# A chunked scan on one core: spilt activations asked for two chunks sooner

## The chip, the cores and the metric

The kernel runs on one core of one Trainium2 chip. The metric is the device time of an execution in microseconds; lower is better. TensorE is called PE here, VectorE DVE, ScalarE ACT, GpSimd POOL and SyncE SP, as in the profile.

## The reference, cut to what matters

A trunk of two layers over 1024 tokens of width 1024, all in float32: a causal spatial-gating layer, then a Mamba-2 SSD layer, then a norm. The change lies in the second layer, whose scan works on 8 groups of 4 heads, in chunks of 128 tokens:

```python
proj = h @ w_in                                   # z | xbc | dt
xbc = silu(causal_depthwise_conv(xbc, conv_w, conv_b))
x, Bm, Cm = split(xbc)                            # in chunks of 128 tokens, 8 groups
dA_cs = cumsum(softplus(dt_raw + dt_bias) * A)    # within a chunk
cb = einsum('bclgn,bcsgn->bclsg', Cm, Bm)
w_ls = cb * exp(dA_cs[l] - dA_cs[s]) (causal) * dt
y_diag = einsum('bclsgj,bcsgjp->bclgjp', w_ls, x)
states = einsum('bclgn,bclgj,bclgjp->bcgjpn', Bm, decay_to_end * dt, x)
prev = scan over chunks: carry * chunk_decay + states
y_off = einsum('bclgn,bcgjpn,bclgj->bclgjp', Cm, prev, exp(dA_cs))
y = y_diag + y_off + x * d_skip
out = rmsnorm_per_group(y * silu(z)) @ w_out      # h = h + out, then the final norm
```

## The kernel before, in words

Large products are made of float32 operands that are split in a high and a low part, three matmuls each (`mm3`, L134 to L136). The order of the work is written out by hand: what stands earlier in the Python text stands earlier on each engine, and a buffer's next user waits for its last reader.

The projections of the second layer come first. For four of the eight groups (`SPILT = (0, 1, 3, 5)`) the convolved x, B and C (`xbc`) are computed ahead of the scan and stored to DRAM, in `xbc_d` of the group, half by half: a **half** is 4 chunks, so there are 16 of them, and half H is group H // 2, with chunks 4H to 4H + 3 in a count n that runs from 0 to 63 over all groups. The projections of the other four groups (`projections`, matmuls into `ab`) are interleaved with the scan as filler: `project` moves them on by a share that grows evenly with n.

`scans` is the loop over the 64 chunks. For each chunk n it puts, in this order: `own` and `off` (PE: this chunk's state and the carried state's part, into `os`), at an even n also `diagonal` for the chunks n and n + 1 (PE, into `yy`) and the loads of the decay matrices `wl` for n + 4 and n + 5 (L1590, on SP; they take the buffers which the diagonal has just read, so they wait for PE), a share of the projections, `pe_a(n + 3)` (PE: three transposes and a product into `tp`, L1595 and L1596, the first that reads a half's `xbc`), then the state's update, the decays (ACT, L1601 and L1603), the weights (DVE, L1619), the skip term (DVE, L1676, of n and n + 1 at an even n), the sum and the gate (POOL, L1689). At a half's end its squares are taken (ACT, L1700), `z` gated is stored (`g_d`, L1704) and a sum of squares is stored (`ss_d`, L1720).

`prefetch(g, th, part)` asks for a half's data on SP's queue. Part 0 is the 1 MB of `xbc` (L1555), for a spilt group only. Part 1 is `ze`: `z` (L1559) and four broadcasts of the decays `ecs_d` (L1563). Part 0 of half H + 1 is asked for at the end of chunk 4H, part 1 at the end of chunk 4H + 1, in which `pe_a` already takes chunk 4H + 4. Both use the pool `s8` with 16 buffers of 8 KB in each partition, which the projections' results, the operands of the products (`hh`, `hl`) and the scan's halves share in turn.

SP issues its DMAs in the order written, and an issue that waits for a buffer holds those behind it. Eight counters of finished DMAs go round, so that a DMA also waits for the one that had its counter before.

The functions that the change touches:

Of the kernel before, what the change touches and what calls it, by code (L numbers as in the profile page):

```python
# [29 lines left out]
def kernel(  # L30
# [34 lines left out]
    def s8(shape, name, dt=F32):  # L65
        return sb.tile(shape, dt, name=name, tag="s8", bufs=16)
# [1244 lines left out]
    def convolve():  # L1311

        finish()
        if todo:
            late.append(todo.pop(0)())
# [75 lines left out]
    def drain(n=1):  # L1391

        for _ in range(min(n, len(queue))):
            for f in queue.pop(0):
                f()
# [153 lines left out]
    def prefetch(g, th, part):  # L1549

        st = sts[g]
        if part == 0:
            if g in xbc_d:
                t = st["xbc", th] = s8([P, 4, 512], "xbc")
                nc.sync.dma_start(out=t, in_=xbc_d[g][:, th])  # L1555
            return
        ze = st["ze", th] = s8([P, 4, 512], "ze")
        if g < G - 1:
            nc.sync.dma_start(out=ze[:, 0:2], in_=z_d[g][:, :, th * 512:(th + 1) * 512])  # L1559
        for f in range(2):  # L1560
            for pt in range(2):
                h = 4 * g + 2 * pt + f
                nc.sync.dma_start(out=ze[f * 64:(f + 1) * 64, 2 + pt],  # L1563
                                  in_=ecs_d[h, th * 512:(th + 1) * 512].partition_broadcast(64))
# [158 lines left out]
    def group_rstd(g, t0, n):  # L1723


        c = n // P
        sv = tiny([P, 8], "sv")[:, 0:c]
        nc.sync.dma_start(out=sv, in_=ss_d[g, t0:t0 + n].rearrange("(p c) -> p c", c=c))
        got = []

        def guess():
            nc.vector.tensor_scalar(sv, sv, 1.0 / 256, NORM_EPS, ALU.mult, ALU.add)
            got.append(rsqrt_a(sv, c))

        def tail():
            rv = tiny([P, 8], "rvv")[:, 0:c]
            rsqrt_b(rv, sv, got[0], c)
            got.append(rv)

        def put():  # L1740
            nc.sync.dma_start(out=rs_d[g, t0:t0 + n].rearrange("(p c) -> p c", c=c), in_=got[1])

        return guess, tail, put
# [117 lines left out]
    def scans():  # L1861


        chunks = [(g, c) for g in range(G) for c in range(8)]
        N, M = len(chunks), 50
        scan, rs, ran = {}, {}, [0]
        total = 32 * len(plain)

        def fill():
            yield from pj  # L1870
            yield from bo.product(1, hook_b)

        fl = fill()

        def project(upto):
            while ran[0] < upto:
                next(fl, None)
                ran[0] += 1

        def want(at):  # L1880
            if at < M:
                return AHEAD + (total - AHEAD) * at // M
            return total + min(16 * (at - M) // (N - 5 - M), 16 + 2 * (at - N + 5))

        def at(f, n, *a):
            if 0 <= n < N:
                g, c = chunks[n]
                if g not in scan:
                    scan[g] = Scan(g, nc.gpsimd)
                getattr(scan[g], f)(c, *a)  # L1890

        prefetch(0, 0, 0), prefetch(0, 0, 1)
        project(AHEAD // 2 + 1)
        while todo or late:
            convolve()
        for n in range(4):
            at("load", n)
        drain(1)
        for n in range(2):
            at("decay", n)  # L1900
        drain(len(queue))
        at("pe_a", 0), at("tokens", 0), at("weights", 0)
        at("pe_a", 1), at("tokens", 1), at("weights", 1)
        drain(len(queue))
        project(AHEAD)
        at("decay", 2)
        at("pe_a", 2), at("tokens", 2)
        for n, (g, c) in enumerate(chunks):
            if n == M + 3:
                drain(len(queue))  # L1910
            elif n == N - 9:
                for k in range(2):
                    bo.get("a", 0, 0, k)
            elif n == N - 7:
                end["scan"] = scan[G - 1]
                bo.get("b", 0, 0, 0)
            p = g if c >= 4 else g - 1
            if c % 2 == 0:
                at("own", n), at("off", n)
                at("diagonal", n)  # L1920
                if c % 4 == 0 and g > 0:
                    scan[g - 1].sum_b()
                elif n == N - 2:
                    scan[g].sum_b(n=2)
                at("load", n + 4), at("load", n + 5)
                project(want(n + .5))
                at("pe_a", n + 3)
                at("update", n)
                at("carry", n + 1)
                at("weights", n + 2)  # L1930
                at("decay", n + 3)
                at("skip", n)
                at("out", n)
                at("skip", n + 1)
                drain()
                at("tokens", n + 3)
                at("gate", n)
                if c % 4 == 0 and g > 0:
                    scan[g - 1].sum_c(1 if c else 0)
                drain()  # L1940
            else:
                at("own", n), at("off", n)
                project(want(n + .5))
                at("pe_a", n + 3)
                at("update", n)
                at("carry", n + 1)
                at("weights", n + 2)
                at("out", n)
                drain()
                at("decay", n + 3)  # L1950
                at("tokens", n + 3)
                at("gate", n)
                drain()
            if n >= N - 7:
                k = n - N + 7
                if k % 2:
                    bo.prep(1, k // 2)
                else:
                    bo.ready(0, 0, k // 2)
            th = 0 if c >= 4 else 1  # L1960
            if p >= 0:
                sc = scan[p]
                if p == G - 1:
                    if c == 4:
                        sc.gate_half(th), sc.squares(th)
                elif c % 4 == 0:
                    sc.squares(th)
                elif c % 4 == 1:
                    sc.store(th)
                    sc.sum_a()  # L1970
            if g > 0:
                if c == 6:
                    rs[g] = group_rstd(g - 1, 0, T)
                elif c == 7:
                    rs[g][0]()
            if c == 0 and g > 1:
                rs[g - 1][1]()
            if c == 1 and g > 1:
                rs[g - 1][2]()
            k = n + 4  # L1980
            if c % 4 < 2 and k < N:
                prefetch(k // 8, k // 4 % 2, c % 4)
            project(want(n + 1))
        sc = scan[G - 1]
        for k in (0, 1):
            bo.get("a", 0, 1, k)
        bo.get("b", 1, 0, 0)
        sc.sum_c(0), rs[G - 1][1](), rs[G - 1][2]()
        bo.prep(1, 3)
        sc.gate_half(1), sc.squares(1)  # L1990
        end["half"] = [group_rstd(G - 1, 0, 512)]
        for k in (0, 1):
            bo.get("a", 1, 0, k)
        while ran[0] < total + 31:
            project(ran[0] + 1)
        sc.sum_b(n=2)
        sc.sum_c(1)
        for _ in fl:
            pass
# [22 lines left out]
    with tc.manual_schedule():  # L2022
        scans()
        into_end()
# [28 lines left out]
```

## Time and profile before

| what | us |
| --- | --- |
| three runs | 1519.4, 1520.2, 1528.06 |
| median | 1520.2 |
| the profiled execution | 1520.27 |
| its span in the trace | 1518.6 |

The span starts with the program's first instruction. The scan's chunks run from about 1007 us (first transposes) to 1346 us (last); the output projection fills the rest. Waits are listed as: engine, line and tile that waited, what it waited for, total us, times, longest. In a timeline a row has start, duration, engine, line, operation, tiles, shapes, and in brackets the idle time of the engine before it and what ended it; `SPq` is an issue on SP's queue. A row of stretches has the stretch, its length, the busy time of PE, PEld (weight load), DVE, ACT and POOL with the instructions in it, the granted PE clock, the DMA engines' share and GB/s.

### The profile page before, as it was taken

What the parts mean: (1) busy time and instruction counts of PE and PEld (TensorE: products, weight loads), DVE (VectorE), ACT (ScalarE), POOL (GpSimd) and SP (SyncE); (2) the same over time, 40 slices, a digit from 0 to 9 for tenths busy, and PEclk for the clock granted to TensorE, in tenths of its full rate; (3) what the DMA queues carried; (4) which work ended last, traced back from release to release, by engine and by line L of the source; (5) the groups of instructions that cost most, each with busy time, mean ns of one, the idle gap of its engine ahead of it and who ended that gap; (6) DMA issues with size and microseconds to landing.
All of it is one profiled execution on the core that took longest, in us unless ns stands there. A gap on an engine that the chain in (4) does not pass through costs nothing. (4 is left out here: it accounts for less than half of the span.)

```text
span 1518.6 us, 21342 instructions
## 1 busy us (share of the span) xinstructions
PE 1463.4 (96%) x7834; PEld 1230.3 (81%) x7834; DVE 1049.1 (69%) x1713; ACT 784.2 (52%) x1256; POOL 402.0 (26%) x451
## 2 busy tenths in 40 slices
PE   6899999999999999999999999998999989999997
PEld 6899988888888888877878888877787878777875
DVE  7966566676666655678657467766677767688876
ACT  6533332232322445556666566565766676756463
POOL 1111110000000023202131313126666676642221
PEclk9999999999999999999999999999999999999999
DMA  5554323322322999948377888776656555589972
GB/s 183 140 169 143 106 89 108 110 105 101 116 87 79 361 247 243 257 133 163 112 174 161 182 169 162 153 235 188 180 145 191 166 181 140 159 264 276 250 162 111
DMA packets 174952, 254.45 MB, mean 168 GB/s; under 512 B 16400, under 2 KB 103168, under 8 KB 171648
## 3 DMA queue, kind: packets, MB, share of 16 engines
q1 hardware_dynamic: 124768, 168.93, 36.0%
q0 software_dynamic: 42448, 70.27, 23.0%
q10 hardware_dynamic: 7632, 13.90, 2.5%
q8 instruction: 62, 1.02, 0.3%
q14 instruction: 42, 0.34, 0.1%
HBM read 186.14 MB, written 51.18 MB: 156 GB/s over the span
## 5 line engine op out<-in xcount | busy, mean ns | idle before, releaser
L134 PE MATMUL acc<-hh,wh 128*128 128x512 f32 x868 | 340.1, 392 | 0.8 <-ACT u L296 0.8
L136 PE MATMUL acc<-hh,wl 128*128 128x512 f32 x868 | 338.5, 390 | 1.9 <-DVE wl L112 1.8
L135 PE MATMUL acc<-hl,wh 128*128 128x512 f32 x868 | 337.8, 389 | 0.0
L112 DVE TENSOR_TENSOR wl<-wr,wh 128x1024 fp32r<-128x1024 f32 (+1 forms) x96 | 114.3, 1192 | 118.7 <-ACT wh L111 118.6
L136 PEld LDWEIGHTS acc<-hh,wl 128*128 128x128 f32 x868 | 162.9, 188 | 37.8 <-DVE wl L112 3.6
L134 PEld LDWEIGHTS acc<-hh,wh 128*128 128x128 f32 x868 | 163.1, 188 | 35.0 <-ACT u L296 1.8
L135 PEld LDWEIGHTS acc<-hl,wh 128*128 128x128 f32 x868 | 163.0, 188 | 33.2
L296 ACT COPY u<-acc 128x512 f32<-128x512 f32 x115 | 66.9, 583 | 197.8 <-PE acc L136 197.7
L111 ACT CAST wh<-wr 128x1024 fp32r<-128x1024 f32 (+1 forms) x112 | 115.2, 1029 | 94.1 <-PE acc L135 56.6
L136 PE MATMUL acc<-wh,hl 128*128 128x256 f32 x448 | 129.2, 288 | 4.4 <-DVE hl L407 4.0
L134 PE MATMUL acc<-wh,hh 128*128 128x256 f32 x448 | 129.6, 289 | 2.4 <-DVE wh L418 1.0
L135 PE MATMUL acc<-wl,hh 128*128 128x256 f32 x448 | 128.6, 287 | 1.3 <-DVE wl L421 1.3
L134 PE MATMUL ab<-hh,wh 128*128 128x512 f32 x288 | 125.0, 434 | 0.8 <-DVE zt L999 0.8
L136 PE MATMUL ab<-hh,wl 128*128 128x512 f32 x288 | 114.2, 397 | 0.0
L135 PE MATMUL ab<-hl,wh 128*128 128x512 f32 x288 | 113.4, 394 | 0.0
L136 PEld LDWEIGHTS acc<-wh,hl 128*128 128x128 f32 x448 | 87.6, 196 | 5.6 <-DVE hl L407 4.7
L134 PEld LDWEIGHTS acc<-wh,hh 128*128 128x128 f32 x448 | 87.7, 196 | 3.4 <-ACT hh L400 1.4
L135 PEld LDWEIGHTS acc<-wl,hh 128*128 128x128 f32 x448 | 87.7, 196 | 1.7 <-DVE wl L421 1.5
L1601 ACT ACTIVATE wl<-wl,tk 128x128 f32<-128x128 f32 x256 | 81.6, 391 | 4.9 <-DMA wl<-cs_d 4.5
L649 POOL DMA_DIRECT2D y_d<-y x8 | 4.4, 549 | 290.6 <-DVE y L646 290.6
L135 PE MATMUL bo<-wl,xh 128*128 128x512 f32 x192 | 75.8, 395 | 5.4 <-DVE wl L112 2.4
L112 DVE TENSOR_TENSOR wl<-t,wh 128x1024 fp32r<-128x1024 f32 (+1 forms) x38 | 45.5, 1196 | 48.3 <-ACT wh L111 48.2
(314 smaller groups left out, 3248.1 us busy)
## 6 DMA issues: line engine op xcount, KB each, us to landing
wr<-in_a_w_in_dram SPq DMA_DIRECT2D x48, 512.0 KB, 3.7
wl<-cs_d SPq DMA_DIRECT2D x64, 256.0 KB, 4.6
wr<-in_b_w_in_dram SPq DMA_DIRECT2D x30, 512.0 KB, 8.4
wb<-in_a_w_out_dram SPq DMA_DIRECT2D x10, 1024.0 KB, 11.8
wb<-in_b_w_out_dram SPq DMA_DIRECT2D x10, 1024.0 KB, 8.9
wr<-in_b_w_in_dram SPq DMA_DIRECT2D x36, 256.0 KB, 6.0
v<-v_d SPq DMA_DIRECT2D x8, 1024.0 KB, 4.7
y_d<-y POOLq DMA_DIRECT2D x8, 1024.0 KB, 5.7
```

Source lines behind the costliest of these rows:

```text
L111: nc.scalar.copy(out=hi, in_=src)
L112: return (eng or nc.vector).tensor_tensor(out=lo, in0=src, in1=hi.bitcast(F32), op=ALU.subtract)
L134: nc.tensor.matmul(out=o, lhsT=l[0], rhs=r[0], start=start, stop=False, **kw)
L135: nc.tensor.matmul(out=o, lhsT=l[0], rhs=r[1], start=False, stop=False, **kw)
L136: nc.tensor.matmul(out=o, lhsT=l[1], rhs=r[0], start=False, stop=stop, **kw)
L296: nc.scalar.copy(out=self.u[n][:, i], in_=a)
L649: store = lambda: nc.gpsimd.dma_start(out=y_d[-1], in_=y)
L1601: nc.scalar.activation(wl[:, j, :], wl[:, j, :], AF.Relu, scale=-1.0, bias=tokc(2, c, self.g)[:, j:j + 1])
```

## The change

Part 0 of a half is asked for at the end of the chunk n for which n + 6 is a half's first chunk, that is at the end of the third chunk of the half two before it; before, it was asked for at the end of the first chunk of the half just before it. Half 1, for which there is no such chunk, is asked for ahead of the scan. Part 1 stays where it was.

```diff
-        prefetch(0, 0, 0), prefetch(0, 0, 1)
+        prefetch(0, 0, 0), prefetch(0, 0, 1), prefetch(0, 1, 0)
...
+            k = n + 6
+            if k % 4 == 0 and k < N:
+                prefetch(k // 8, k // 4 % 2, 0)
             k = n + 4
-            if c % 4 < 2 and k < N:
-                prefetch(k // 8, k // 4 % 2, c % 4)
+            if c % 4 == 1 and k < N:
+                prefetch(k // 8, k // 4 % 2, 1)
             project(want(n + 1))
```

Only SP's queue is put in another order. These are the rows of SP ahead of the scan and at its first chunk, before (-) and now (+). `xbc_d_6209` is the spill of group 0; `wr` are weights of the projections.

```order
 L1559 DMA ze<-z_d_5287 128x2x512
 L1563 DMA ze<-ecs_d 64x512 x4
+L1555 DMA xbc<-xbc_d_6209 128x2048
 L120 DMA wr<-in_b_w_in_dram 128x4x256
 L1590 DMA wl<-cs_d 128x512 x4
 L120 DMA wr<-in_b_w_in_dram 128x4x256
 L1590 DMA wl<-cs_d 128x512 x2
-L1555 DMA xbc<-xbc_d_6209 128x2048
 L1559 DMA ze<-z_d_5287 128x2x512
```

The request for half 1 moved from behind the loads of chunk 0 to ahead of the weight load and of the `wl` loads for chunks 0 to 3.

Next, SP around chunks 6 and 8, where half 3 (the second of group 1, whose spill is `xbc_d_6210`) is asked for. The first two `wl` loads are those of chunk 6, the other two those of chunk 8; the tile `g_d` has another number in the changed program.

```order
 L120 DMA wr<-in_b_w_in_dram 128x4x128 x2
-L1590 DMA wl<-cs_d 128x512 x4
-L1720 DMA ss_d<-gsq 2x256
+L1590 DMA wl<-cs_d 128x512 x2
 L1555 DMA xbc<-xbc_d_6210 128x2048
-L1704 DMA g_d_8254<-ze 256x1x512
+L1590 DMA wl<-cs_d 128x512 x2
+L1720 DMA ss_d<-gsq 2x256
+L1704 DMA g_d_8256<-ze 256x1x512
```

The request moved ahead of the `wl` loads of chunk 8 and of the `ss_d` store that it stood behind.

Last, SP around chunks 38 and 40, where half 11 (the second of group 5, spill `xbc_d_6212`) is asked for, with the semaphores that each issue waits for; `sv` is a load for a group's norm, at chunk 38.

```order
 L1728 DMA sv<-ss_d 128x8
-L120 DMA wr<-in_b_w_in_dram 128x4x256 [waits DMAHW3_49]
-L1590 DMA wl<-cs_d 128x512 [waits DMAHW4_49,DVE_49,PE_49]
-L1590 DMA wl<-cs_d 128x512 [waits DMAHW5_49,DVE_49,PE_49]
-L1720 DMA ss_d<-gsq 2x256 [waits DMAHW6_49,Activation_49]
-L1555 DMA xbc<-xbc_d_6212 128x2048 [waits DMAHW7_49]
+L1555 DMA xbc<-xbc_d_6212 128x2048 [waits DMAHW3_49,DVE_49]
+L120 DMA wr<-in_b_w_in_dram 128x4x256 [waits DMAHW4_49]
+L1590 DMA wl<-cs_d 128x512 [waits DMAHW5_49,PE_49,Activation_49]
+L1590 DMA wl<-cs_d 128x512 [waits DMAHW6_49,DVE_49,PE_49]
+L1720 DMA ss_d<-gsq 2x256 [waits DMAHW7_49,Activation_49]
 L1704 DMA g_d_9939<-ze 256x1x512 [waits DMAHW0_49,Pool_49]
```

The request moved ahead of a weight load, the next two `wl` loads and the `ss_d` store, and it now also waits for DVE, whose skip term is the last reader of the buffer that it takes.

## The prediction

> **What bounds the kernel now.** I began with the page's first part, which gives the engines' shares of the span.
>
> ```profile
> PE 1463.4 (96%) x7834; PEld 1230.3 (81%) x7834; DVE 1049.1 (69%) x1713; ACT 784.2 (52%) x1256; POOL 402.0 (26%) x451
> ```
>
> TensorE (PE) is busy for nearly all of the span, so a change that leaves its work alone can win only what it idles. The list of waits on PE, narrowed to the scan of groups 0 to 5 (1000 to 1290 us), has one row; its columns are total us, times, longest. The second row is the largest from the same list for 1290 us to the end.
>
> ```profile
> PE tp L1595 <- DMA xbc<-xbc_d: 15.5, 7, 2.9
> PE bo L135 <- DVE wl L112: 2.4, 4, 1.0
> ```
>
> In the scan PE waits for nothing but spilt activations: seven times, 15.5 us in all, at the first transposes of a half whose `xbc` has just been asked for. Behind the scan it is the same PE that leads (`bo`, the output projection), with waits of 2.4 us at most. So I take what PE wins in the scan to reach the end one for one.
>
> The timeline shows one of the seven whole, first SyncE's queue (SP), then PE.
>
> ```profile
> 1239.03 0.80 SPq L1590 DMA_DIRECT2D wl<-cs_d  x2
> 1242.14 0.50 SPq L1720 DMA_DIRECT2D ss_d<-gsq  x1
> 1242.69 0.38 SPq L1555 DMA_DIRECT2D xbc<-xbc_d  x1
> ```
>
> ```profile
> 1245.24 0.40 PE L136 MATMUL ab<-hh,wl 128*128 128x512 f32 x1
> 1248.58 0.68 PE L1595 MATMUL tp<-ident,xbc 128*128 128x128 f32 x3 [2.94 <-DMA xbc<-xbc_d]
> 1250.77 0.63 PE L134 MATMUL ab<-hh,wh 128*128 128x512 f32 x1
> 1251.20 0.63 PE L135 MATMUL ab<-hl,wh 128*128 128x512 f32 x1
> 1252.05 0.47 PE L134 MATMUL ab<-hh,wh 128*128 128x512 f32 x1
> 1252.36 0.39 PE L135 MATMUL ab<-hl,wh 128*128 128x512 f32 x1
> 1252.59 0.40 PE L136 MATMUL ab<-hh,wl 128*128 128x512 f32 x1
> ```
>
> The request leaves at 1242.69, behind the `wl` loads and the `ss_d` store of chunk 40; PE is ready for chunk 44 just after 1245.24. The request's landing time (view of line 1555, us from issue) decides:
>
> ```profile
> DMA to landing us min/median/max: 5.8/6.4/7.1
> ```
>
> At 5.8 us or more, a request 2.6 us ahead of its reader must be late.
>
> **The change part by part.** No engine gets or loses an instruction: eight requests of 1 MB stay eight, and PE, VectorE (DVE), ScalarE (ACT) and GpSimd (POOL) keep their order. Half 1's request moves to the start, the six later ones (halves 2, 3, 6, 7, 10, 11) up by two chunks on SP.
>
> *The idle time that goes.* 15.5 us by the list. An idle time counts from a modelled end, so I add what that hides: 1245.24 to 1248.58 is 3.34 us start to start, and a step there takes 0.24 us without a wait:
>
> ```profile
> 1068.20 0.39 PE L136 MATMUL ab<-hh,wl 128*128 128x512 f32 x1
> 1068.44 0.49 PE L1595 MATMUL tp<-ident,xbc 128*128 128x128 f32 x3
> ```
>
> That is 3.10 lost against 2.94 listed, 0.16 more each time; 15.5 + 7 x 0.16 = 16.6 us.
>
> *The slow stretch behind two of them.* Above, 1250.77 to 1251.20 is 0.43 us for a matmul of 512 columns; from 1252.36 to 1252.59 the same takes 0.23. The stretches of the same place (PE, PEld, DVE, ACT, POOL busy, then granted clock) say why, and show a second place:
>
> ```profile
> 1250.00:1252.00 2.00, 2.00 (x6) 1.57 (x5) 0.35 (x2) 1.57 (x4) 1.71 (x3) 0.50 0.38 116
> 1076.00:1078.00 2.00, 2.00 (x6) 1.53 (x6) 0.62 (x2) 1.99 (x5) 1.32 (x3) 0.50 1.00 172
> 1060.00:1090.00 30.00, 28.01 (x175) 23.03 (x176) 18.19 (x37) 19.64 (x39) 18.02 (x23) 0.94 0.51 145
> 1240.00:1270.00 30.00, 27.06 (x158) 22.32 (x158) 19.16 (x44) 17.76 (x41) 19.71 (x22) 0.94 0.58 173
> ```
>
> The granted clock is 0.50 after the waits that end at 1248.58 and 1074.79, and these two stretches of 30 us are the only ones of the scan below 1.00. From 1248.58 to 1252.05 PE ran 3.47 us at half rate and did what takes about 1.9 us (3.47 x 0.23 / 0.43): 1.6 us lost, 3.2 for the two. The Trainium skill ("TensorE: Matmul & The Clock Gate", Part 1 on the HAM clock gate) says that the clock falls to half after an idle window of about 3.4 us, and in its section on HAM oscillation puts the rule as no idle gap over that. The trace differs: the second place idled 1.99 us (row below). By that rule these gaps would not have cost the clock; what this would make of the sum is a rival below.
>
> ```profile
> 1028.77 0.55 PE L1595 MATMUL tp<-ident,xbc 128*128 128x128 f32 x3 [2.86 <-DMA xbc<-xbc_d]
> 1074.79 0.87 PE L1595 MATMUL tp<-ident,xbc 128*128 128x128 f32 x3 [1.99 <-DMA xbc<-xbc_d]
> ```
>
> So 16.6 + 3.2 = 19.8 us go if all seven waits go. A second way to the same: SP's `wl` loads at the first chunk of a half are released by PE, so their distance is a half's length. Those of chunks 12, 16, 20, 24, 44 and 48 (40 is at 1239.03 above):
>
> ```profile
> 1089.61 1.73 SPq L1590 DMA_DIRECT2D wl<-cs_d  x2
> 1109.77 0.81 SPq L1590 DMA_DIRECT2D wl<-cs_d  x2
> 1130.82 0.85 SPq L1590 DMA_DIRECT2D wl<-cs_d  x2
> 1153.76 0.79 SPq L1590 DMA_DIRECT2D wl<-cs_d  x2
> 1264.81 0.80 SPq L1590 DMA_DIRECT2D wl<-cs_d  x2
> 1285.00 0.81 SPq L1590 DMA_DIRECT2D wl<-cs_d  x2
> ```
>
> The two halves from chunk 12 have no such wait: 20.16 and 21.05 us (a second half of a group, then a first); the second half from chunk 44 has none either, 20.19. The half from chunk 20 has one: 22.94, which is 2.78 more than 20.16. The half from chunk 40 (1239.03 to 1264.81) takes 25.78, 4.73 more than 21.05; its own rows give 2.94 + 0.16 + 1.6 = 4.70. So a half without the wait really runs at the undisturbed length, and the other engines keep up with that pace over two halves in a row.
>
> *Does the earlier request land in time?* For half 11 it now stands behind the loads of chunk 38 (`wl`, `sv`), for half 3 behind those of chunk 6:
>
> ```profile
> 1056.05 0.81 SPq L1590 DMA_DIRECT2D wl<-cs_d  x2
> 1232.50 0.42 SPq L1728 DMA_DIRECT2D sv<-ss_d  x1
> ```
>
> Half 3: issued about 1056.9, landed by 1064.0 at the slowest 7.1, wanted just after 1072.4 (1074.79 less 1.99 and a matmul): 8 us to spare. Half 11: issued about 1233, landed by 1240.1, wanted at 1245.6: 5.5 to spare. Each earlier removed wait brings the request forward with its reader, since SP's queue there is paced by PE.
>
> *What the request waits for now.* It needs a free buffer one half sooner, which adds a wait in five of the six places; behind it on SP stand the `wl` loads of the next chunk but one, then `ss_d` and `g_d` stores. Half 3 waits for ACT's squares (L1700) of half 0, halves 6 and 10 for such squares too; half 7 and half 11 for DVE's skip term (L1676) of the last chunk of the group before.
>
> ```profile
> 1043.99 1.05 ACT L1700 ACTIVATE gsq<-ze 128x1024 f32<-128x1024 f32 x1
> 1231.84 0.59 DVE L1676 SCALAR_TENSOR_TENSOR cw<-x,dsk,yy 128x128 f32<-128x128 f32 x2
> ```
>
> The squares end at 1045.0, 11.9 us ahead of half 3's new request; the skip term ends at 1232.4, before SP is through with `sv` at 1232.9. I cost these waits at nothing. If DVE were later, say by 3 us, half 11 would still have 2.5 us, and the weight load (`wr`) now behind it belongs to the projections' next product, several chunks off.
>
> *The start.* Half 1's megabyte now goes ahead of a weight load and of the `wl` loads of chunks 0 to 3, where the DMA engines are full (share 0.92 and 0.84, then 0.35; the other columns as above):
>
> ```profile
> 1000.00:1005.00 5.00, 5.00 (x23) 4.13 (x22) 2.20 (x5) 0.82 (x1) 0.85 (x1) 1.00 0.92 335
> 1005.00:1010.00 5.00, 5.00 (x29) 4.25 (x27) 2.73 (x8) 1.64 (x3) 0.00 (x0) 1.00 0.84 266
> 1010.00:1015.00 5.00, 5.00 (x24) 4.14 (x23) 2.82 (x3) 4.54 (x8) 0.00 (x0) 1.00 0.35 105
> ```
>
> ```profile
> 1004.80 10.21 SPq L1590 DMA_DIRECT2D wl<-cs_d  x4
> 1011.97 1.27 ACT L1601 ACTIVATE wl<-wl,tk 128x128 f32<-128x128 f32 x4
> ```
>
> At 335 GB/s a megabyte takes 3.1 us. The first `wl` is asked for at 1004.80 and read by ACT at 1011.97, 7.2 us later, against 3.9 us to land (the one load that the view of DMAs gives whole):
>
> ```profile
> wl<-cs_d SPq DMA_DIRECT2D x1, 256.0 KB, 3.9
> ```
>
> So 3.3 us are free, and 3.1 fits. The cost lies between nothing (a faster start is excluded: nothing there is asked for sooner but this) and 7.1 - 3.3 = 3.8 us, if the whole slowest landing stood ahead of `wl`. I take 0.5, near the 3.1. The megabyte itself, asked for near 1004, has landed long before its reader at 1028.77.
>
> *What is late next.* The transposes also need a PSUM slot; for half 11 its last reader is ACT's copy of the group's sum, for which the `ss_d` store waits that leaves at 1242.14, 3.5 us before PE is there. ACT is full at the second stall (1.99 of 2.00 us from 1076), which is the case for the first rival. I add nothing.
>
> Sum against the profiled execution's own time, 1520.27 us (span 1518.6 and 1.7 around it): 1520.27 - 19.8 + 0.5 = **1501.0 us**. The median of the runs, 1520.2, is the same within 0.1.
>
> **The rivals.**
> - *Stalls traded.* With PE earlier, a follower is late: ACT is full around the second stall. Half of the 19.3 us comes back: 1520.27 - 9.7 = 1510.6. Against it: the two undisturbed halves at full pace, and no other row in the list of waits.
> - *The slow clock has another cause and stays.* Then only 16.6 - 0.5 = 16.1 us go: 1504.2. For it: the wait of 2.86 us at 1028.77, longer than one of the two, left no stretch below 1.00. Against it: both slow stretches stand straight behind a wait. The Trainium skill's rule cited above ("TensorE: Matmul & The Clock Gate") would have it so.
> - *It doesn't do what it says.* The request is held by its buffer until where it stood: 1520. Against it: the two rows above, both done before SP arrives.
> - *Slower.* The megabyte follows straight on the two `wl` loads of the half's third chunk and shares the DMA engines with them, and ACT needs the first of these within the next chunk. ACT already waited for `wl` once behind such a pair:
>
> ```profile
> 1046.14 1.28 ACT L1601 ACTIVATE wl<-wl,tk 128x128 f32<-128x128 f32 x4 [1.11 <-DMA wl<-cs_d]
> ```
>
>   If `wl` landed with the slowest request (7.1 instead of 3.9) and PE waited it out, 3.2 x 7 = 22.4 us return and the kernel takes 1523. It decides from 2.8 us per half (19.3 / 7). Against it: the same pair stands ahead of the same megabyte now, two chunks later, and PE's list has no wait from it.
>
> **How the numbers follow.** A measurement of this kernel can tell about 1%, 15 us, from no change. Full gain: 0.70, between 1498 (the sum without its start cost, 1500.5, less 2.5 for the runs' spread and small waits near the stalls) and 1505. Clock rival 0.06. Stalls traded 0.16, some 1504 to 1516. Not as it says 0.04. Slower 0.04. The range 1498 to 1509 leaves out most of the last three and little else, about 2 in 10. Faster by over 1% (under 1505.0): nearly all of the first, most of the second and a tenth of the third, 0.74. Within 1%: 0.23. Slower by over 1%: 0.03.
>
> **What will show it.** PE's list should have no `xbc` row, the granted clock no 0.50 in the scan; the `wl` loads at first chunks should stand 20 to 21 us apart throughout; `xbc` requests should leave right behind the third chunk's `wl` loads and land 5 us or more ahead of their transposes. The forecast is wrong if PE waits at `yy` or `os` instead, if ACT's waits for `wl` grow by microseconds per half, or if the first `yy` comes over 1 us later than now.

## The result, and the profile after

| | before | changed |
| --- | --- | --- |
| median | 1521.36 us (4 runs) | 1500.66 us (4 runs, 1500.03 to 1501.1) |
| profiled execution, its span | 1520.27, 1518.6 us | 1500.63, 1498.9 us |

The ratio is 0.9856 with a 95% interval of 0.9825 to 0.9887: faster by 1.4%. The profiled executions differ by 19.64 us, the medians by 20.7; the prediction said 19.3. (The kernel before had medians of 1521 to 1525 us in the groups of runs that follow, so each experiment is compared with the runs of before beside it.)

PE's list of waits from 985 to 1290 us has lost the row of 15.5 us. Both rows left belong to work ahead of the scan:

```profile
PE acc L136 <- DVE wl L112: 1.3, 1, 1.3
PE ab L134 <- DVE zt L999: 0.7, 1, 0.7
```

The two stretches of 30 us that stood at a granted clock of 0.94 (the third figure from the end) stand at 1.00, and PE is busy through all of both:

```profile
1060.00:1090.00 30.00, 30.00 (x186) 24.82 (x183) 21.36 (x45) 22.72 (x46) 19.94 (x23) 1.00 0.56 177
1240.00:1270.00 30.00, 30.00 (x195) 24.67 (x194) 22.65 (x48) 22.64 (x47) 21.49 (x25) 1.00 0.46 128
```

SP's queue shows the `wl` loads issued at chunks 20, 24, 32, 36, 40 and 44 and, between them, the new place of a request (half 11, behind the `sv` load of chunk 38):

```profile
1122.01 0.82 SPq L1590 DMA_DIRECT2D wl<-cs_d  x2
1142.22 0.80 SPq L1590 DMA_DIRECT2D wl<-cs_d  x2
...
1183.42 0.80 SPq L1590 DMA_DIRECT2D wl<-cs_d  x2
1204.47 0.81 SPq L1590 DMA_DIRECT2D wl<-cs_d  x2
...
1217.25 0.42 SPq L1728 DMA_DIRECT2D sv<-ss_d  x1
1218.11 0.32 SPq L1555 DMA_DIRECT2D xbc<-xbc_d  x1
1224.69 0.79 SPq L1590 DMA_DIRECT2D wl<-cs_d  x2
...
1245.71 0.80 SPq L1590 DMA_DIRECT2D wl<-cs_d  x2
```

The half from chunk 20, 22.94 us before, takes 20.21; that from chunk 36, 20.22; that from chunk 40, 25.78 before, 21.02. From chunk 8 to chunk 48 every half now has one of the two undisturbed lengths, 20.2 or 21.0 us within 0.1. The reader of half 11, in PE's timeline, is no longer late and runs at full rate (0.49 us for three transposes, 0.68 before):

```profile
1231.10 0.49 PE L1595 MATMUL tp<-ident,xbc 128*128 128x128 f32 x3
```

The request left 13 us ahead of it; for the other five the lead is 13.8 to 16.2 us.

### The profile page after: what moved, and what is told of

Its sections match the earlier page's. It is cut to its first block, busy times and chain, and to the rows that moved or that the text cites. A ratio compares the mean times of both kernels' runs of the same rounds, so it can differ in the third digit from the quotient of the medians.

```text
span 1498.9 us, 21344 instructions
## 1 busy us (share of the span) xinstructions
PE 1458.9 (97%) x7834; PEld 1228.7 (82%) x7834; DVE 1045.8 (70%) x1713; ACT 783.6 (52%) x1256; POOL 401.2 (27%) x451
```

## The experiments

The theory: PE's waits at the transposes, and the slow clock behind some of them, are all of the gain. Its rivals: the gain comes from splitting a burst of transfers; the slow clock has another cause; the lead in chunks counts rather than the place on SP's queue.

### The two parts alone

Each diff is against the kernel before or the changed kernel, as named with it. Half 1 alone, against the kernel before:

```diff
-        prefetch(0, 0, 0), prefetch(0, 0, 1)
+        prefetch(0, 0, 0), prefetch(0, 0, 1), prefetch(0, 1, 0)
...
-            if c % 4 < 2 and k < N:
+            if c % 4 < 2 and k < N and k != 4:
```

> Only half 1 is asked for ahead of the scan; the six later requests stand where they stood before. Theory (PE's waits): the first of the seven waits goes, 2.86 + 0.16 us, less some 0.3 at the start, so about 2.7 us below the kernel before, 1517.5. Rival (traffic: the time comes from splitting the burst of transfers at a half's first chunk, and PE's waits only mark it): one burst of seven is split, but a megabyte is added to full DMA engines at the start, so no gain, 1520.

Measured: 1519.23 us beside 1523.48, ratio 0.997 (0.9957 to 0.9983), 4.6 us with an interval of 2.6 to 6.6, which just takes in the 2.7 expected. In the profile six waits are left, 12.3 us, 3.2 less; the first is gone:

```profile
PE tp L1595 <- DMA xbc<-xbc_d: 12.3, 6, 3.0
```

The six later ones alone, against the changed kernel:

```diff
-        prefetch(0, 0, 0), prefetch(0, 0, 1), prefetch(0, 1, 0)
+        prefetch(0, 0, 0), prefetch(0, 0, 1)
...
+            if n == 0:
+                prefetch(0, 1, 0)
             k = n + 6
```

> Half 1 is asked for where it was before, the six later ones two chunks sooner. Theory (PE's waits): one wait of 2.9 us stays, the rest goes: 19.8 - 3.0 = 16.8 us below the kernel before, 1503.5; the first transposes of half 1 wait as before and nothing else in the scan does. Rival (the start's full DMA engines cost as much as the first wait): the same time as the changed kernel, 1500.7, or below.

Measured: 1505.15 us, ratio 0.9883 (0.9866 to 0.9901), 17.8 us less than before. One wait is left, and a slow clock follows it (0.50 in the stretch of 2 us below):

```profile
1028.15 0.55 PE L1595 MATMUL tp<-ident,xbc 128*128 128x128 f32 x3 [2.97 <-DMA xbc<-xbc_d]
```

```profile
1030.00:1032.00 2.00, 2.00 (x7) 1.63 (x7) 0.77 (x1) 1.95 (x6) 0.78 (x2) 0.50 0.16 49
```

So the parts add up (4.6 + 17.8 = 22.4 us against 21.8 in the next run, which has both), and the start does not eat the first wait's gain. The traffic rival fails on the first: it had no gain there.

### One chunk sooner, and three

Both diffs are against the changed kernel.

```diff
-            k = n + 6
+            k = n + 5
```

> The later six are asked for one chunk sooner instead of two, at the end of a half's fourth chunk. Theory (the place on SP's queue counts, since the loads of an even chunk are what PE holds up): the request still stands ahead of the decay loads of the next half's first chunk, in the same place of SP's queue as in the changed kernel, so the same time, 1500.7 within 1 us, with no wait for spilt activations. Rival (the lead in chunks counts): half the lead, about half the gain, 1510.

Measured: 1502.86 us in the same group, ratio 0.9857 (0.9836 to 0.9879), the changed kernel's 0.9856. PE's list has no `xbc` row:

```profile
PE acc L136 <- DVE wl L112: 1.3, 1, 1.3
PE ab L134 <- DVE zt L999: 1.2, 1, 1.2
```

The place on SP's queue counts: ahead of the `wl` loads that PE releases. The second chunk of lead adds nothing, since SP reaches both places at nearly the same time: counted from the `wl` loads ahead of it, the request leaves within 0.14 us of the changed kernel's in five of six halves. At half 11 it leaves 2.2 us later, and still 10.8 us ahead of its reader.

```diff
-            k = n + 6
+            k = n + 7
```

> The later six are asked for three chunks sooner, at the end of a half's second chunk, one more than in the changed kernel. Theory (PE's waits): none is left to win, 1500.7 within 1 us, unless SP is held at the request. Rival (the buffer's wait): the request now waits for a half's stored gate and squares while the decay loads stand behind it; if that holds them up, decays are late and PE waits at the diagonal products, 1 us or more in each of two halves, 1503 or more.

Measured: 1503.76 us beside 1522.77, ratio 0.9877 (0.9862 to 0.9892). The intervals overlap with the changed kernel's, so by time alone a loss is not shown; the profile shows what the rival said. PE has a new wait, ACT's wait for `wl` is 15.7 us where it is 3.3 in the changed kernel, and SP is held at the request by a gate store (the last row, SP's own list):

```profile
PE tp L1595 <- DVE state L1663: 1.9, 2, 1.4
ACT wl L1601 <- DMA wl<-cs_d: 15.7, 8, 3.7
SPq L1555 <- DMA g_d<-ze: 8.7, 2, 6.1
```

How it reaches PE, at half 7: the request leaves at 1130.38, the loads behind it late, and DVE stands 4 us at a norm's `sv` with the state's copy behind it, for which PE's transposes wait. PE loses 0.45 of the 1.9 us here, and 1.42 at half 11, where DVE stands 3.7 us at such an `sv`.

```profile
1130.38 0.34 SPq L1555 DMA_DIRECT2D xbc<-xbc_d  x1
1134.67 0.58 SPq L1559 DMA_DIRECT2D ze<-z_d  x1
...
1138.96 0.60 SPq L1728 DMA_DIRECT2D sv<-ss_d  x1
```

```profile
1143.48 0.17 DVE L1732 TENSOR_SCALAR sv<-sv 128x8 f32<-128x8 f32 x1 [4.01 <-DMA sv<-ss_d]
1143.56 0.42 DVE L1663 COPY state<-os 128x256 f32<-128x256 f32 x1
```

### A smaller lead, and fewer waits without moving a request

The request directly behind the `wl` loads of the half's first chunk, against the kernel before:

```diff
                 at("load", n + 4), at("load", n + 5)
+                if c % 4 == 0 and n + 4 < N:
+                    prefetch((n + 4) // 8, (n + 4) // 4 % 2, 0)
...
-            if c % 4 < 2 and k < N:
-                prefetch(k // 8, k // 4 % 2, c % 4)
+            if c % 4 == 1 and k < N:
+                prefetch(k // 8, k // 4 % 2, 1)
```

> The kernel before with one step: the request stands directly behind the decay loads of the half's first chunk, ahead of the weight loads and of the store of the group's sum. It leaves sooner by about 0, 1.0, 0.7, 1.7, 2.4, 1.4 and 2.9 us (halves 1, 2, 3, 6, 7, 10, 11). Theory (PE's waits): each wait shrinks by that lead or goes, 0 + 1.0 + 0.7 + 1.7 + 1.25 + 1.12 + 2.9 = 8.6 us, and 1.6 more if the slow clock at half 11 goes with its wait: 1510 to 1512. Rival (traffic): the burst stays together, no gain, 1520.

Measured: 1518.66 us beside 1523.48, ratio 0.9972 (0.9957 to 0.9987), 4.3 us: half of what was expected. The waits shrank by 4.7 us, not 8.6:

```profile
PE tp L1595 <- DMA xbc<-xbc_d: 10.8, 7, 2.9
```

At half 10 the request left at 1217.20 and the transposes began at 1225.39, 8.2 us later; in the kernel before (the last two rows) it was 1219.76 to 1226.62, 6.9 us.

```profile
1217.20 0.42 SPq L1555 DMA_DIRECT2D xbc<-xbc_d  x1
```

```profile
1225.39 0.52 PE L1595 MATMUL tp<-ident,xbc 128*128 128x128 f32 x3 [1.07 <-DMA xbc<-xbc_d]
```

```profile
1219.76 0.39 SPq L1555 DMA_DIRECT2D xbc<-xbc_d  x1
```

```profile
1226.62 0.52 PE L1595 MATMUL tp<-ident,xbc 128*128 128x128 f32 x3 [1.12 <-DMA xbc<-xbc_d]
```

My expectation kept the landing time fixed. It grew as the request moved up to the `wl` loads; that they share the DMA engines is the likely reason, which no run isolates. Time still follows the waits, and the traffic rival, which gave no gain, fails here too.

PE's side alone: the kernel before, with SP's queue as it was and the filler moved.

```diff
-                project(want(n + .5))
+                project(want(n + (1 if c % 4 == 1 else .5)))
                 at("pe_a", n + 3)
```

> The kernel before with SP's queue as it was; in the second chunk of each half, PE does that chunk's whole share of the projections ahead of the transposes, not half of it. The transposes come some six matmuls, 1.4 us, later. Theory (PE's waits): each wait shrinks by 1.4 or goes, 1.4 x 5 + 1.25 + 1.12 = 9.4 us, up to 3.2 more if the shorter waits no longer cost the clock: 1508 to 1511. Rival (traffic): no request moves, no gain, 1520.

Measured: 1513.23 us beside 1522.77, ratio 0.994 (0.9922 to 0.9959), 9.1 us. Waits at the transposes are 8.0 us in five places, 7.5 less, and new small waits of 1.6 stand at the diagonal products:

```profile
PE tp L1595 <- DMA xbc<-xbc_d: 8.0, 5, 2.2
PE yy L1630 <- DVE wl L1619: 1.6, 3, 0.9
```

The net of these, 5.9 us, lies just under the interval of the gain, 6.2 to 11.9, so the waits need not be all of it. No request moved, and the kernel is faster: this speaks most plainly against the traffic rival.

### The slow clock

The changed kernel with halves 3 and 11, or 2 and 6, asked for at the old place:

```diff
             k = n + 6
-            if k % 4 == 0 and k < N:
+            if k % 4 == 0 and k < N and k // 4 not in (3, 11):
                 prefetch(k // 8, k // 4 % 2, 0)
             k = n + 4
+            if k % 4 == 0 and k // 4 in (3, 11):
+                prefetch(k // 8, k // 4 % 2, 0)
```

> The changed kernel with the requests of halves 3 and 11 back where they were; these are the two whose waits were followed by a slow clock. Theory: their waits return, 1.99 + 2.94 + 0.32 = 5.3 us, and with them a slow stretch each, 3.2 us: 1509.2. Rival (the slow clock is not tied to the place but to when the wait falls): the waits alone, 1506.0, or one slow stretch, 1507.6.

> The changed kernel with the requests of halves 2 and 6 back where they were; these waits were of the same length as the others (2.78 and 2.53 us) but no slow clock followed. Theory (slow clock tied to the place): the waits alone, 2.78 + 2.53 + 0.32 = 5.6 us, 1506.3, granted clock 1.00. Rival (tied to when the wait falls): one or two slow stretches as well, 1507.9 or 1509.5.

Measured: 1509.22 and 1509.78 us beside 1522.77, ratios 0.9912 (0.9895 to 0.9928) and 0.9914 (0.9899 to 0.9929); at 0.9856 the changed kernel would take 1500.8 there, so 8.4 and 9.0 us returned. The clock is not tied to the place: of halves 3 and 11 only the longer wait brought a slow stretch, though a long one (1235.64 to 1242.47, two of the usual length), and half 2, which had none before, brought one now. Halves 3 and 11, both waits and the stretches behind the longer:

```profile
1069.36 0.52 PE L1595 MATMUL tp<-ident,xbc 128*128 128x128 f32 x3 [2.20 <-DMA xbc<-xbc_d]
1236.88 0.88 PE L1595 MATMUL tp<-ident,xbc 128*128 128x128 f32 x3 [3.78 <-DMA xbc<-xbc_d]
```

```profile
1236.00:1238.00 2.00, 1.12 (x6) 1.16 (x7) 0.00 (x0) 0.00 (x0) 0.00 (x0) 0.50 0.36 123
1238.00:1240.00 2.00, 2.00 (x6) 1.61 (x6) 0.62 (x2) 1.09 (x2) 1.23 (x2) 0.50 0.25 56
1240.00:1242.00 2.00, 2.00 (x6) 1.52 (x6) 0.00 (x0) 1.94 (x6) 2.00 (x3) 0.50 0.79 283
1242.00:1244.00 2.00, 2.00 (x14) 1.65 (x14) 0.04 (x1) 0.00 (x0) 1.64 (x1) 0.88 0.83 178
```

Halves 2 and 6, the wait of half 2 and the stretch behind it:

```profile
1052.15 0.52 PE L1595 MATMUL tp<-ident,xbc 128*128 128x128 f32 x3 [3.27 <-DMA xbc<-xbc_d]
```

```profile
1054.00:1056.00 2.00, 2.00 (x6) 1.53 (x6) 0.87 (x1) 2.00 (x6) 2.00 (x3) 0.50 1.13 183
```

Next, each wait longer: a quarter of a half's data is loaded once more ahead of the request, in the kernel before and in the changed one.

```diff
                 t = st["xbc", th] = s8([P, 4, 512], "xbc")
+                if (g, th) != (0, 0):
+                    nc.sync.dma_start(out=t[:, 0], in_=xbc_d[g][:, th, 0])
                 nc.sync.dma_start(out=t, in_=xbc_d[g][:, th])
```

> The kernel before, with a quarter of each half's activations (256 KB, halves 1 to 11) loaded once more ahead of the whole request, which waits for it to land: every request lands some 3 us later. Theory (PE's waits, and a slow clock the more surely the longer the wait): seven waits grow by 3 us each, 21 us, to between 4 and 6; all were above 2.9, from which every wait so far brought a slow clock, so seven slow stretches where there were two, 5 x 1.6 = 8 us: 1520 + 29 = 1549. Rival (a wait's length does not decide on the clock): four stretches of seven as among the waits of 2 to 2.9 us, 1544 or less, with granted clock 1.00 behind some waits of 4 us.

Measured: 1552.43 us beside 1524.74, ratio 1.0184 (1.0168 to 1.0201), 28 us more. The waits grew by 20.4 us, and the transposes behind each of the seven ran slow (0.81 to 0.88 us where 0.49 to 0.55 is normal). The list of waits, then the longest and the shortest in the timeline:

```profile
PE tp L1597 <- DMA xbc<-xbc_d: 35.9, 7, 7.0
```

```profile
1060.52 0.87 PE L1597 MATMUL tp<-ident,xbc 128*128 128x128 f32 x3 [6.97 <-DMA xbc<-xbc_d]
1252.65 0.81 PE L1597 MATMUL tp<-ident,xbc 128*128 128x128 f32 x3 [3.74 <-DMA xbc<-xbc_d]
```

The rest, 28 - 20.4 = 7.6 us (5.2 to 10.2 by the interval), is what the slow clock adds. It is not five more stretches of one length: four of the seven are twice as long as the two before, 6.83 us against 3.41. From the transposes' starts on, PE ran 28.8 us at 0.50, against 6.8 in the kernel before, 22.1 more. At the prediction's price, 1.6 us for 3.41, that is an estimate of 10.4 us; the two profiled executions, 30.65 us apart, leave 10.25.

The changed kernel with the same load:

> The changed kernel with the same quarter loaded once more ahead of each request, halves 1 to 11, so that each lands some 3 us later. Theory (5 us or more to spare at every reader): nothing is waited for, 1500.7 within 1.5 us. Rival (the spare time is used up, or SP is held while the small load lands, so that the decay loads behind it are late): waits of 1 us or more at the transposes or the diagonal products, 1505 or more.

Measured: 1503.08 us beside 1524.74, ratio 0.9862 (0.9845 to 0.988). No transposes wait for `xbc`. One new wait stands at the scan's start (`os`, 1.5 us). It has the form of the rival, on a small scale: SP is held 2.9 us while the small load lands, so the first `wl` loads leave 4.3 us behind half 1's first load, not 1.9, and ACT waits for them 2.42 us, not 0.59:

```profile
PE os L1640 <- ACT cw L1615: 1.5, 1, 1.5
```

```profile
1013.97 1.28 ACT L1603 ACTIVATE wl<-wl,tk 128x128 f32<-128x128 f32 x4 [2.42 <-DMA wl<-cs_d]
```

The extra load that costs 28 us where the reader stands close costs nothing that shows in the time where there are 13 us or more for it.

## Why the prediction was right, point by point

- **Idle time, 16.6 us.** All seven waits went, and no other took their place in PE's list. Both parts alone, the smaller lead and the moved filler show time following these waits.
- **The two terms together, 19.8 us.** They can be read in the scan itself, from its first transposes (1007.28, now 1008.07) to those of the last group's `bc`, first before, then now:

```profile
1311.16 0.33 PE L1595 MATMUL tp<-ident,bc 128*128 128x128 f32 x1 [1.04 <-ACT bc L1433]
1292.07 0.33 PE L1595 MATMUL tp<-ident,bc 128*128 128x128 f32 x1 [1.04 <-ACT bc L1433]
```

  That is 303.88 and 284.00 us, 19.9 less. That the whole came as near as 19.64 to 19.3 is partly luck: this execution reached the scan 0.8 us later, and won 0.6 behind it; neither was forecast.
- **Slow clock, 3.2 us.** Shown by the runs: it comes behind waits at the transposes and is gone from the scan without them, and the 1.6 us for one stretch fits what the longer waits cost. The rival that gave it another cause falls. The theory that tied it to two places, which I tested later, falls as well: which waits bring a stretch hangs on where they fall in time (last section), so two of seven holds for the profiled execution, and others can have had more or fewer.
- **Start, 0.5 us.** Own products and diagonal of chunk 0, the first two rows before, the others now:

```profile
1018.48 0.60 PE L1638 MATMUL os<-cw 128*128 128x256 f32 x2
1019.01 1.10 PE L1630 MATMUL yy<-wl,cw 128*64 128x128 f32 x16
1019.27 0.67 PE L1638 MATMUL os<-cw 128*128 128x256 f32 x2
1019.87 1.26 PE L1630 MATMUL yy<-wl,cw 128*64 128x128 f32 x16
```

  The diagonal starts 0.86 us later, the product ahead of it 0.79, and the scan's first transposes already 0.8 (1008.1 against 1007.3): some 0.1 at the diagonal, so 0.5 was too much. ACT did wait 0.59 us for the first `wl`: the 3.3 us of slack, which were worked out to be just enough, were used up, and a little more:

```profile
1013.92 1.28 ACT L1601 ACTIVATE wl<-wl,tk 128x128 f32<-128x128 f32 x4 [0.59 <-DMA wl<-cs_d]
```

- **Landing in time.** Right, with a figure that was too small: "7.1 at the slowest" came from the landing row, but in the kernel before half 2 left at 1043.94 and its transposes, which waited for it, began at 1052.41, 8.5 us later:

```profile
1043.94 0.60 SPq L1555 DMA_DIRECT2D xbc<-xbc_d  x1
```

```profile
1052.41 0.52 PE L1595 MATMUL tp<-ident,xbc 128*128 128x128 f32 x3 [2.78 <-DMA xbc<-xbc_d]
```

  With 13 us of lead it did not matter; in the run with the smaller lead the same habit, a fixed landing time, made the forecast twice the gain.
- **The buffers' waits, nothing.** Right in effect. In SP's list five of the requests are held, 4.6 us in all and 1.5 at most, half 11 for 0.4 by the skip term that was to be done in time; none of it reaches PE. One chunk earlier two are held for 8.7 us, and it does.
- **The slower rival.** ACT's waits for `wl` in the scan went from 3.7 to 3.3 us, the new 0.59 at the start included, so the megabyte behind the pair of loads cost ACT nothing.

No version tried beats the changed kernel: one chunk sooner is the same, three chunks and the others are not faster.

## What to carry to other kernels

On a queue that issues in order, a prefetch's lead is set by the nearest issue ahead of it that waits for the busy engine, not by how many iterations early it is written: look for that issue and put the request ahead of it, and no further than its buffer is free, since a held request holds all that is behind it. Size the lead by the time from issue to the reader's start in the trace at that place, not by a landing time from a quieter one. And price a TensorE stall with the slow clock that may follow: here 1.6 us for each 3.41 us at half the clock, behind waits as short as 1.99 us.

## What the runs showed of the hardware that I had not expected

A wait of 1.99 us was enough to cost the clock. Over the kernel before and the seven experiments that kept waits for `xbc`, a stretch at 0.50 followed all 14 waits of 2.9 us or more, 4 of the 10 between 1.9 and 2.9 us (as short as 1.99, and not 2.86), and none of the 13 below.

The length alone does not decide. Read in stretches of 0.2 us, the profiles show that each slow stretch behind such a wait lasts 3.41 us, or twice that. Start and end of one in the kernel before, 1248.80 to 1252.21:

```profile
1248.60:1248.80 0.20, 0.20 (x2) 0.20 (x3) 0.00 (x0) 0.00 (x0) 0.00 (x0) 1.00 1.17 440
1248.80:1249.00 0.20, 0.20 (x3) 0.20 (x2) 0.00 (x0) 0.00 (x0) 0.00 (x0) 0.51 0.82 273
1252.20:1252.40 0.20, 0.20 (x3) 0.16 (x2) 0.00 (x0) 0.20 (x2) 0.20 (x1) 0.96 0.96 369
```

Within a run the starts lie on one grid. In the kernel before with the longer waits they are 1030.88, 1058.18, 1085.49, 1157.17, 1184.48, 1252.74 and 1276.64, all whole numbers of steps of 3.413 us apart, to 0.01 us. Laid over the waits of its run, the grid sorts all 37: the 18 that a slow stretch followed filled 1.92 us or more of a single step, the 19 others 1.83 at most. So the wait of 1.99 us cost the clock because 1.92 of it fell into one step, and that of 2.86 did not because it was split, 1.03 and 1.83. The clock falls at the end of such a step. It comes back after one step, or after two where the wait also takes 1.14 us or more of the next (five stretches, one of them behind the wait of 3.78 us). The bounds are those of these runs, with idle time as the profile lists it.

The Trainium skill ("TensorE: Matmul & The Clock Gate", Part 1 on the HAM clock gate) tells of an activity window of about 3.4 us that runs freely. The steps of 3.41 us agree with that. The rule that the Trainium skill gives in the section on HAM oscillation of the same page, no idle gap over about 3.4 us, does not agree as a limit: the gap that filled 1.92 us of a step was enough.
